# Ordering the program of a two-layer hybrid backbone by another model of the engines

## The chip, the cores and the metric

The kernel runs on one core of one Trainium2 chip. A core has a matrix engine (TensorE, PE in the profile), three engines for element-wise work (VectorE or DVE, ScalarE or ACT, GpSimd or POOL), a queue for data transfers (SyncE, SP) and 16 DMA engines. Each engine works through its own list of instructions in the order in which the program puts them there; semaphores hold an instruction back until what it reads has been written. The metric is the device time of one execution in microseconds (us). Times are compared with the median of several runs.

## What is computed

Two layers are applied to 256 latent tokens and 256 context tokens of width 1024 (batch 1), in fp32. Each layer is a half-step SwiGLU FFN, a token mixer and another half-step FFN; every sub-layer is modulated (adaLN) by vectors that come from a condition vector and a large matrix `ada_w`.

```python
for l in range(DEPTH):                                     # DEPTH = 2
    mx = (silu(c) @ ada_w[l] + ada_b[l])                   # 9 modulation vectors per stream
    x = x + 0.5 * mx[2] * swiglu(ada_norm(x, norm_g[l, 0], mx[0], mx[1]), ffn_w_in[l, 0], ffn_w_out[l, 0])
    # the same for the context stream hctx
    hx, hc = ada_norm(x, ..., mx[3], mx[4]), ada_norm(hctx, ...)
    yx, yc = even_mixer(hx, hc, ...) if l % 2 == 0 else odd_mixer(hx, hc, ...)
    x = x + mx[5] * yx
    x = x + 0.5 * mx[8] * swiglu(ada_norm(x, norm_g[l, 2], mx[6], mx[7]), ffn_w_in[l, 1], ffn_w_out[l, 1])
    # the same for hctx, but not in the last layer
return rms_norm(x, final_g)
```

The even mixer is differential attention with 4 heads beside a bidirectional mLSTM with 4 heads; the odd mixer is bidirectional gated linear attention (GLA) with 4 heads. The hidden width of an FFN is 2816.

## The kernel before

The two token streams lie side by side as columns 0 to 255 (context) and 256 to 511 (latent) of tiles with 128 features in the partitions, so that most matmuls have 512 columns. Every large product is done in three passes over split numbers: a weight tile and an activation tile are each cut into a rounded high part and a rest, and `mm3` adds high x high, high x rest and rest x high into one bank (L146, L147, L148).

The stages follow each other in the code: `begin` (loads, transposes of the tokens, first modulation vectors), the first FFN, the even mixer, two FFNs, the odd mixer, the last FFN with the final norm.

How the work of a stage reaches the engines:

- `load` (L116) issues a 1 MB transfer of weights from SP's queue into one of three `raw` buffers. `ada_step` (L167) uses the same three buffers for quarters of `ada_w`.
- `split` cuts half of such a buffer: ACT copies it, rounded, into `whi` (L120), DVE subtracts that from the raw values into `wlo` (L121). There are two buffers of each, so ACT can begin on a half only when PE is done with the half before the last.
- In an FFN, `ffn_in` goes through 22 tiles of hidden features in pairs; for each tile PE does 48 matmuls from two halves, and `gated` forms silu(a) x b (ACT at L348 and L350, DVE at L349 and L351). After each pair, `ada` calls `ada_step` twice: eight multiply-adds of 128 x 1024 on DVE (L176, L178). `out_pass` does the second product of the FFN and calls `ada_step` once for each raw buffer. The calls stop when the 64 steps (16 units of modulation vectors by 4 quarters) are done.
- `norm_steps` and `modulate` form the normalised activations `hh` and `hl` for the next stage (ACT, DVE, and POOL at L275).
- The even mixer runs the gate chain of the mLSTM (L759 to L790: activations on ACT, scans on DVE, transposes by PE at L784), then the heads: scores, weights, their transposes (`wtrans`, L894), the product with the values (`pv`, L907), a norm, and the transpose of the result (L916). `stack` (L841 to L847) lays out queries and keys for the scores. Between the heads stand projections that are independent of them (`rows_pair` with L632 to L634, `qk_pair`, `opre_pair`).
- The odd mixer does the same with `decays` (transposes at L1202), `states` and `head_out` (products at L1258 and L1260, transposes at L1267).

What sets the order of the work: the code is traced once, and when the block `with tile.TileContext(...)` closes, a list scheduler puts the traced instructions into the queues. It goes through a modelled execution, and whenever an engine of the model is to get an instruction, it takes, of those whose inputs are there and whose buffers are free at that moment of the model, the one that stands first in the code. So an instruction can pass others of its engine that stand ahead of it in the code but are not ready by the model. It also hands out the buffers of a pool as the instructions come up. Semaphore waits are put in after that, and keep the result right whatever the order. Only `keep_in_program_order` (L107), used for loads of the activation tables, ties an instruction to the one traced before it on its engine. No cost, due time or priority is written by hand.

## Time and profile before

| what | us |
|---|---|
| median of 3 runs | 1805.3 |
| lowest and highest | 1801.82 and 1805.34 |
| the profiled execution | 1805.46 |
| its span, first to last instruction | 1803.8 |

The profiled execution takes 1.7 us more than its span, for what lies around the program's own instructions. The profile's page is made from this one execution. Its mean granted PE clock is 0.995.

How to read it: a row of a group names the line of the kernel, the engine, the operation, and what it writes and reads (out<-in, buffer numbers left out), then the count, the busy time and the mean duration of one. "SPq" is SP's queue, in which an issue of a transfer can wait. A wait is put down to the engine whose result came last. PE's ends are modelled, and successive matmuls overlap in the rows, so that start-to-start distances say more of its pace than durations do.

The transfers are large and many, and in these rows of the page (line, engine, count, KB each, us from issue to landing) the largest are seen:

```profile
raw<-in_ffn_w_in_dram SPq DMA_DIRECT2D x84, 1024.0 KB, 5.3
raw_ada<-in_ada_w_dram SPq DMA_DIRECT2D x64, 1024.0 KB, 5.0
raw<-in_ffn_w_out_dram SPq DMA_DIRECT2D x41, 1024.0 KB, 5.0
```

The lines on which the argument rests stand in the prediction.

### The profile page before, as it was taken

The page shows a single profiled execution, that of the slowest core. Times are in us where ns is not written, and L with a number is a line of the kernel's source. Part 1 is how long each engine was busy: PE and PEld are TensorE (multiplying, and loading weights), DVE is VectorE, ACT ScalarE, POOL GpSimd, SP SyncE. Part 2 cuts the span into 40 slices and gives each one's busy share as a digit, 9 for nine tenths or more (in the row PEclk, how much of TensorE's full clock was granted, in tenths as well). Part 3 has the DMA queues.
Part 4 walks back from the last instruction along what each step waited for, and adds up shares of the span by engine and source line. Part 5 has one row for each costly group of instructions (what it writes and reads, how often), then busy time and mean ns, then how long its engine had stood idle before and what let it go on. Part 6 is the DMA issues. An engine that isn't in the chain of part 4 may idle for free.

```text
span 1803.8 us, 24901 instructions
## 1 busy us (share of the span) xinstructions
PE 1765.4 (98%) x10087; PEld 1503.6 (83%) x10087; DVE 1153.9 (64%) x1678; ACT 743.3 (41%) x1286; POOL 107.1 (6%) x172
## 2 busy tenths in 40 slices
PE   8999999999999999999999999999999999999998
PEld 5777778899887788777788897777888998899996
DVE  5767775657669866677753486777543747855555
ACT  4422222237658853222222352222222656654443
POOL 1000000013011020000000010000000200010000
PEclk9999999999999999999999999999999999999999
DMA  9555545443121214555542344555443632235553
GB/s 295 177 187 179 177 158 192 164 132 122 47 71 47 94 48 140 182 175 182 184 142 97 129 141 163 187 187 187 140 133 101 189 117 71 89 106 191 186 190 117
DMA packets 209303, 262.30 MB, mean 145 GB/s; under 512 B 6863, under 2 KB 188662, under 8 KB 209188
## 3 DMA queue, kind: packets, MB, share of 16 engines
q1 hardware_dynamic: 208160, 259.28, 44.0%
q8 instruction: 79, 1.29, 0.3%
q0 software_dynamic: 576, 0.84, 0.2%
q10 hardware_dynamic: 452, 0.59, 0.1%
q14 instruction: 36, 0.29, 0.1%
HBM read 259.64 MB, written 1.05 MB: 145 GB/s over the span
## 4 chain that ended last, share of the span: by engine, by line
PE 85%; DVE 7%; ACT 4%; issue 2%; DMA 1%; SPq 0%; POOL 0%; ACTq 0%; POOLq 0%; DVEq 0%
PE ps_ab L146 16%; PE ps_ab L147 16%; PE ps_ab L148 16%; PE ps_y L146 7%; PE ps_y L148 7%; PE ps_y L147 7%; PE ps_fm L148 2%; PE ps_fm L146 2%; PE ps_fm L147 2%; DVE wlo L121 1%; PE po L907 1%; PE ada_ps L190 1%; PE ps_l L1382 1%; PE ps_l L1383 1%; PE ps_l L1381 1%
## 5 line engine op out<-in xcount | busy, mean ns | idle before, releaser
L120 ACT CAST whi<-raw 128x1024 fp32r<-128x1024 f32 (+1 forms) x326 | 336.0, 1031 | 849.7 <-PE ps_ab L147 497.3
L121 DVE TENSOR_TENSOR wlo<-raw,whi 128x1024 fp32r<-128x1024 f32 (+1 forms) x326 | 392.6, 1205 | 314.4 <-ACT whi L120 309.5
L146 PE MATMUL ps_ab<-hh,whi 128*128 128x512 f32 (+1 forms) x1360 | 491.3, 362 | 1.8 <-ACT whi L120 1.0
L147 PE MATMUL ps_ab<-hl,whi 128*128 128x512 f32 (+1 forms) x1360 | 490.4, 361 | 2.6 <-POOL hl L275 2.3
L148 PE MATMUL ps_ab<-hh,wlo 128*128 128x512 f32 (+1 forms) x1360 | 489.4, 360 | 0.4 <-DVE wlo L121 0.3
L178 DVE SCALAR_TENSOR_TENSOR acc<-raw_ada,cs,acc 128x1024 f32<-128x1024 f32 x224 | 276.5, 1280 | 42.8 <-DMA raw_ada<-in_ada_w_dram 42.8
L146 PEld LDWEIGHTS ps_ab<-hh,whi 128*128 128x128 f32 x1360 | 255.4, 188 | 50.1 <-ACT whi L120 6.3
L147 PEld LDWEIGHTS ps_ab<-hl,whi 128*128 128x128 f32 x1360 | 255.9, 188 | 46.0 <-POOL hl L275 2.9
L148 PEld LDWEIGHTS ps_ab<-hh,wlo 128*128 128x128 f32 x1360 | 255.7, 188 | 44.0 <-DVE wlo L121 1.0
L148 PE MATMUL ps_y<-gh,wlo 128*128 128x512 f32 (+1 forms) x660 | 229.9, 348 | 0.4
L146 PE MATMUL ps_y<-gh,whi 128*128 128x512 f32 (+1 forms) x660 | 230.0, 348 | 0.0
L147 PE MATMUL ps_y<-gl,whi 128*128 128x512 f32 (+1 forms) x660 | 228.8, 347 | 0.0
L148 PEld LDWEIGHTS ps_y<-gh,wlo 128*128 128x128 f32 x660 | 124.9, 189 | 17.7 <-DVE wlo L121 1.6
L349 DVE TENSOR_TENSOR s<-ps_ab,s 128x512 f32<-128x512 f32 (+1 forms) x88 | 54.7, 623 | 132.6 <-PE ps_ab L148 131.1
L146 PEld LDWEIGHTS ps_y<-gh,whi 128*128 128x128 f32 x660 | 124.9, 189 | 17.1 <-ACT whi L120 1.2
L147 PEld LDWEIGHTS ps_y<-gl,whi 128*128 128x128 f32 x660 | 124.9, 189 | 15.5
L257 POOL TENSOR_TENSOR ssum<-ssum,sq 128x256 f32<-128x256 f32 x25 | 26.2, 1049 | 1117.8 <-ACT sq L255 842.2
L146 PE MATMUL ps_fm<-hh,whi 128*128 128x256 f32 (+1 forms) x256 | 83.8, 327 | 0.0
L148 PE MATMUL ps_fm<-hh,wlo 128*128 128x256 f32 (+1 forms) x256 | 83.2, 325 | 0.0
L147 PE MATMUL ps_fm<-hl,whi 128*128 128x256 f32 (+1 forms) x256 | 82.9, 324 | 0.0
L632 PE MATMUL ps_v<-whi,hh 128*128 128x256 f32 x256 | 73.4, 287 | 1.3 <-ACT mv L636 1.3
L633 PE MATMUL ps_v<-wlo,hh 128*128 128x256 f32 x256 | 73.9, 289 | 0.0
(375 smaller groups left out, 2383.4 us busy)
## 6 DMA issues: line engine op xcount, KB each, us to landing
raw<-in_ffn_w_in_dram SPq DMA_DIRECT2D x84, 1024.0 KB, 5.3
raw_ada<-in_ada_w_dram SPq DMA_DIRECT2D x64, 1024.0 KB, 5.0
raw<-in_ffn_w_out_dram SPq DMA_DIRECT2D x41, 1024.0 KB, 5.0
raw<-in_even_w_in_dram SPq DMA_DIRECT2D x12, 1024.0 KB, 5.3
raw<-in_odd_w_in_dram SPq DMA_DIRECT2D x12, 1024.0 KB, 5.4
raw<-in_ffn_w_out_dram SPq DMA_DIRECT2D x15, 768.0 KB, 4.3
raw_c<-in_ada_w_dram SPq DMA_DIRECT2D x16, 512.0 KB, 7.4
raw<-in_even_w_out_dram SPq DMA_DIRECT2D x4, 1024.0 KB, 5.0
```

The source lines that it names most:

```text
L120: nc.scalar.copy(hi3, r3)
L121: eng.tensor_tensor(lo3, r3, hi3.bitcast(F32), ALU.subtract)
L146: nc.tensor.matmul(ps, lhsT=wh, rhs=ah, start=first, stop=False)
L147: nc.tensor.matmul(ps, lhsT=wh, rhs=al, start=False, stop=False)
L148: nc.tensor.matmul(ps, lhsT=wl, rhs=ah, start=False, stop=last)
L178: nc.vector.scalar_tensor_tensor(ada_acc[i], r3[:, k2], s, ada_acc[i], ALU.mult, ALU.add)
L190: nc.tensor.matmul(ps[32 * j : 32 * j + 32, :256], lhsT=unit_e[:, 2 * (n - first) + i], rhs=acc[i][:, j * 256 : j * 256 + 256], start=n == ...
L257: (nc.gpsimd if i and k < KC - 2 else nc.vector).tensor_tensor(ssum[i][0], ssum[i][0], sq, ALU.add)
L349: nc.vector.tensor_tensor(s[:, sl], ps[1][:, sl], s[:, sl], ALU.mult)
L632: nc.tensor.matmul(o, lhsT=ah, rhs=wh[:, k4], start=k == 0 and t % 2 == 0, stop=False)
L633: nc.tensor.matmul(o, lhsT=ah, rhs=wl[:, k4], start=False, stop=False)
L907: nc.tensor.matmul(po[:, t], lhsT=w[:, kt, (t % 2) * P : (t % 2) * P + P], rhs=v[:, kt, h * P : h * P + P], start=kt == 0, stop=kt == nk - 1,)
```

## The change

`TileContext` is given `schedule_with_timeline_sim=True`. The list scheduler then goes through its modelled execution on another model of the core: the timeline model, in which each instruction is a series of steps (decoding, waiting in the engine's queue, executing, its result and its semaphore landing later) that hold parts of an engine for their own times, in place of the core model, in which an instruction takes its engine for one length of time. When an instruction is ready, and when its engine can take it, comes out at other moments, and so may the order of the instructions within each engine's queue and the buffer that a tile is given. The instructions themselves, their shapes and the numbers they compute stay the same.

```diff
@@ -1445,7 +1445,7 @@
             nc.dram_tensor(f"in_{name}_dram", a.shape, mybir.dt.from_np(a.dtype), kind="ExternalInput").ap()
         )
     args.append(nc.dram_tensor("out_0_dram", _OUT, F32, kind="ExternalOutput").ap())
-    with tile.TileContext(nc) as tc:
+    with tile.TileContext(nc, schedule_with_timeline_sim=True) as tc:
         backbone_kernel(tc, *args)
     r = _run(nc, [arrays], core_ids=[0])
     return r.results[0]["out_0_dram"].reshape(1, T, D)
```

## The prediction

> **What bounds the kernel now.** First the page: the span, the busy times, and the chain of work that ended last.
>
> ```profile
> span 1803.8 us, 24901 instructions
> PE 1765.4 (98%) x10087; PEld 1503.6 (83%) x10087; DVE 1153.9 (64%) x1678; ACT 743.3 (41%) x1286; POOL 107.1 (6%) x172
> PE 85%; DVE 7%; ACT 4%; issue 2%; DMA 1%; SPq 0%; POOL 0%; ACTq 0%; POOLq 0%; DVEq 0%
> ```
>
> TensorE (PE) is busy for 1765.4 of 1803.8 us and carries 85% of the chain. No order of the same instructions can win more than the 38.4 us in which PE does nothing, and that is 2.1%. So I next ask where these 38.4 us lie, with the view of busy time by stretches (columns: length, then busy time of PE, PEld, DVE, ACT and POOL, the granted PE clock, the DMA share and GB/s).
>
> ```profile
> 0.00:50.00 50.00, 41.81 (x255) 30.35 (x259) 27.23 (x73) 20.17 (x42) 4.99 (x23) 0.93 1.05 297
> 50.00:400.00 350.00, 350.00 (x1687) 282.69 (x1680) 230.96 (x262) 103.36 (x138) 5.52 (x5) 1.00 0.51 169
> 400.00:700.00 300.00, 286.46 (x1902) 255.38 (x1901) 228.88 (x493) 202.82 (x464) 47.50 (x70) 0.99 0.25 78
> 700.00:1000.00 300.00, 300.00 (x1354) 239.98 (x1353) 180.00 (x194) 81.78 (x105) 3.28 (x3) 1.00 0.48 159
> 1000.00:1100.00 100.00, 98.83 (x649) 90.13 (x648) 63.30 (x82) 44.09 (x71) 10.20 (x10) 1.00 0.43 143
> 1100.00:1400.00 300.00, 300.00 (x1366) 240.94 (x1366) 177.02 (x194) 81.54 (x107) 5.07 (x5) 1.00 0.47 154
> 1400.00:1700.00 300.00, 292.85 (x2325) 279.71 (x2324) 191.50 (x316) 164.61 (x298) 27.91 (x55) 1.00 0.42 133
> 1700.00:1750.00 50.00, 50.00 (x366) 47.46 (x366) 26.99 (x32) 24.00 (x32) 0.00 (x0) 1.00 0.54 188
> 1750.00:1804.00 54.00, 45.46 (x200) 36.99 (x198) 28.01 (x39) 20.93 (x32) 2.64 (x2) 0.97 0.37 135
> ```
>
> The four FFN stretches (50 to 400, 700 to 1000, 1100 to 1400, 1700 to 1750) are 1000 us with no idle PE at all. The idle time is 8.2 us at the start, 13.5 us around the even mixer (400 to 700), 1.2 us at 1000 to 1100, 7.2 us around the odd mixer (1400 to 1700) and 8.5 us at the end. The third view, PE's waits, says what the mixers wait for: first 400 to 700, then 1400 to 1700 (columns: total us, times, longest).
>
> ```profile
> PE pmt L784 <- DVE t L781: 3.3, 1, 3.3
> PE pt L894 <- DVE ea L974: 2.2, 2, 1.4
> PE pt_o L916 <- DVE on L913: 1.6, 2, 1.4
> ...
> PE pt L894 <- DVE E L882: 1.1, 3, 0.4
> PE ptg L1202 <- DVE kd L1178: 2.9, 5, 0.9
> PE po L1260 <- ACT st L1249: 1.3, 2, 0.8
> ...
> PE pt_o L1267 <- DVE on L1263: 0.2, 1, 0.2
> ```
>
> These are the links of the heads' own chains: PE wants a transpose or a product, and the DVE or ACT result before it is not there. Everything else in the mixers is covered: while one head's link is under way, PE has projection matmuls of other heads to run.
>
> **The change part by part.** No instruction, tile or shape is added or removed; what moves is the order in each engine's queue and, with it, which instruction gets a shared buffer first. So the sum has one kind of term: waits that go and waits that come, stage by stage.
>
> *FFN stretches, 1000 us.* The timeline of DVE, ACT and PE here:
>
> ```profile
> 149.30 4.87 DVE L178 SCALAR_TENSOR_TENSOR acc<-raw_ada,cs,acc 128x1024 f32<-128x1024 f32 x4
> 154.09 1.21 DVE L121 TENSOR_TENSOR wlo<-raw,whi 128x1024 fp32r<-128x1024 f32 x1
> 146.48 1.05 ACT L120 CAST whi<-raw 128x1024 fp32r<-128x1024 f32 x1 [4.04 <-issue]
> 152.08 1.05 ACT L120 CAST whi<-raw 128x1024 fp32r<-128x1024 f32 x1 [3.99 <-PE ps_ab L147]
> 152.07 0.40 PE L146 MATMUL ps_ab<-hh,whi 128*128 128x512 f32 x1
> 152.53 0.40 PE L148 MATMUL ps_ab<-hh,wlo 128*128 128x512 f32 x1
> ```
>
> One half-tile of weights costs PE 5.60 us (152.08 - 146.48, one cast per half). The cast at 152.08 fills the buffer for the half that starts 5.60 us later, at 157.68, and its wlo is first read 0.46 us into that half (152.53 - 152.07), at 158.14. The wlo ends at 155.30 although four adaLN multiply-adds (4.87 us) stood in front of it. That leaves 2.84 us: two more multiply-adds (1.22 us each) may slip in front without PE noticing, a third may not. Lower end: below nothing is excluded, because PE has no idle time here to give. Upper end: four further multiply-adds in front, 4.87 - 2.84 = 2.0 us for each of the 64 adaLN steps (16 units by 4 quarters in the code), 130 us. I take 0, since the rows nearest to this, today's, already have a whole step of four in front and still 2.84 us in hand.
>
> SP's queue of loads moves too, if the buffers come free in another order:
>
> ```profile
> SPq L116 <- DVE wlo L121: 844.2, 127, 22.3
> ```
>
> SP stands waiting for a raw buffer nearly half of the time, so it issues a load as soon as there is room, and the loads have no other input to wait for. The DMA share is about half (0.47 to 0.51 above). I take 0 for it; if a weight load came one adaLN step late (4.87 us), the same 2.84 us would cover more than half.
>
> *Start and end, 16.7 us idle.* The start waits for loads and the end is one dependent chain behind the last matmul; neither has other ready work to put in between. I take 0, with ends of -2 and +2 us (a quarter of the start's 8.2 us).
>
> *The mixers.* In the code a head of the even mixer has three transposes of weights (L894) and one of the output (L916), with 8 heads 32 links; the odd mixer has 8 transposes at L1202, 4 products at L1260 and 4 transposes at L1267, 16 links. Of the 48, the rows above show 15 that wait (2 + 2 + 3 + 5 + 2 + 1) for 2.2 + 1.6 + 1.1 + 2.9 + 1.3 + 0.2 = 9.3 us, 0.62 us each. The other 33 are covered. Another model places the filling matmuls elsewhere. Lower end: all 15 are covered, -9.3 us. Upper end: all 48 are bare, 33 x 0.62 = +20.5 us. I take half of them bare, 24 of 48: 9 more than now, 9 x 0.62 = +5.6 us. Why half: the order is fixed before the run, and at each link the real times differ from the modelled ones by some tenths of a us, in one direction or the other, so that a link is late about as often as early; today's 15 of 48 is better than that, and a new order has 33 links to lose and 15 to win.
>
> One wait can be traced to an order that is visibly unlucky. The gate chain of the mLSTM (L760 to L781) ends in the 3.3 us wait at L784:
>
> ```profile
> 443.75 0.69 ACT L760 ACTIVATE t<-psg,gb 64x512 f32<-64x512 f32 x1
> 444.46 0.62 ACT L845 CAST stk<-mq 64x512 fp32r<-64x512 f32 x1
> 445.10 0.63 ACT L761 ACTIVATE t<-t 64x512 f32<-64x512 f32 x1
> 445.76 0.62 ACT L844 CAST stk<-mq 64x512 fp32r<-64x512 f32 x1
> 446.40 0.72 ACT L762 ACTIVATE t<-t,one_t 64x512 f32<-64x512 f32 x1
> ...
> 450.00:455.00 5.00, 2.25 (x19) 2.04 (x18) 4.82 (x7) 1.57 (x2) 0.12 (x1) 1.00 0.00 0
> 455.00:460.00 5.00, 4.46 (x23) 4.27 (x24) 3.84 (x8) 2.06 (x7) 0.40 (x1) 0.66 0.00 0
> ```
>
> Two copies that the gate chain does not need (0.62 us each) stand between three links of it: 1.2 us of the wait is order, and the new order may keep or drop them. Both ends, 0 and -1.2; I take 0, for the timeline shows no reason why another model would not fill the same gaps. The last two rows are stretches: after the wait PE was granted 0.66 of its clock for 5 us, which costs (1 - 0.66) x 5 = 1.7 us more. This is the one place in the mixers where a wait costs more than its length.
>
> [...]
>
> **The sum** is 0 + 0 + 5.6 = +5.6 us on the profiled execution. Its own time is 1805.5 us, 1.7 us around the span, and that is the median of the runs shown (1805.3). Forecast: 1811 us.
>
> **The rivals.**
> *Better cover (faster).* The times of the timeline model are nearer to the engines' own, and the mixers' links are covered. All 15 waits and the 1.2 us of the gate chain go: 1805.5 - 9.3 - 1.2 = 1795 us; with the clock dip too, 1793. For it: most waits are under 1 us, the size of a wrong estimate of one DVE operation. Against it: 33 links of 48 are already right.
>
> *Nothing that can be measured.* The new order differs in places that are covered, or is the old one: 1805.5 us. For it: 1000 us without idle PE, and 2.8 us in hand at each half. Against it: the rows of the gate chain show copies written far behind it in the code standing inside it, so the order does hang on modelled times to tenths of a us. Of changes within 0.2% (3.6 us) a measurement of this kernel can't tell whether they are there; its three runs differ by that much.
>
> *The adaLN work runs ahead (slower).* If the timeline model lets ready instructions into DVE's queue before DVE is free, two adaLN steps stand in front of a wlo: eight multiply-adds where four stand now, and PE waits 2.0 us (worked out above). It decides from the third extra multiply-add on. At a quarter of the 64 steps that is 16 x 2.0 = 32 us, 1838 us; at an eighth 1822. For it: DVE is busy for 231 of 350 us in the first FFN stretch, the most of all engines beside PE. Against it: three raw buffers are shared by weights and adaLN, so two adaLN loads are seldom in at once. [...]
>
> **How the numbers follow.** Forecast (half of the links bare, 1809 to 1817): 0.30. Better cover (1790 to 1802): 0.30. Nothing that can be measured: 0.22. AdaLN ahead (1820 and more): 0.18. Faster by over 0.2%: 0.30; within: 0.22; slower: 0.30 + 0.18 = 0.48. The likeliest single case and the likelier side agree on slower, but the cases of the other sign hold much: its own range is 1809 to 1817. The range for 8 in 10 goes from 1791 to 1838: it leaves out the far ends of the two outer cases, about a tenth on each side, since each may be wider than I could price it.
>
> **What would show it.** Right: the FFN stretches still have 300 of 300 and 350 of 350 us of PE; PE's idle time at 400 to 700 and 1400 to 1700 rises from 20.7 to about 26 us; the waits at L894, L916, L1202 and L1260 become more in number, not longer. Wrong towards faster: fewer than 15 such waits, and no copies (L844, L845) between L760 and L762. Wrong towards slower: PE waiting for wlo L121 or whi L120 in ps_ab, in runs of about 2 us, with eight multiply-adds of L178 in a row ahead; or a granted clock under 1 in more stretches than the one above. The forecast falls altogether if the loads on SP's queue come in another order and PE waits for raw.

## The result, and the profile after

| | us | runs |
|---|---|---|
| before | 1805.32 (1801.82 to 1805.62) | 4 |
| after | 1886.34 (1882.53 to 1890.53) | 4 |
| ratio | 1.0453 (1.044 to 1.0466) | |

The changed kernel is 81 us slower. The forecast was +5.6 us, and the time lies far outside the range. The profiled execution of the changed kernel took 1887.84 us. Its page (span, busy times, chain of work that ended last):

```profile
span 1886.1 us, 24938 instructions
PE 1796.1 (95%) x10087; PEld 1526.4 (81%) x10087; DVE 1157.2 (61%) x1678; ACT 744.6 (39%) x1286; POOL 107.9 (6%) x172
PE 81%; DVE 8%; DMA 4%; ACT 3%; issue 2%; SPq 1%; POOL 0%; DVEq 0%; POOLq 0%; ACTq 0%
```

The instruction counts of the engines are those of before. The span grew by 82.3 us, in two parts: PE is busy for 30.7 us more with the same 10087 matmuls (1796.1 - 1765.4), and it does nothing for 51.6 us more (90.0 against 38.4). DVE's and ACT's busy times are the same to 3.3 and 1.3 us. The stretches say where; their bounds are moved so that each ends at nearly the same point of the work as in the table of before (columns as there; by the matmuls counted, to within some 30 of them):

```profile
0.00:50.00 50.00, 36.92 (x227) 27.37 (x227) 24.86 (x66) 18.68 (x38) 4.98 (x23) 0.90 0.99 279
50.00:410.50 360.50, 358.53 (x1714) 286.91 (x1711) 231.06 (x268) 104.78 (x139) 7.07 (x5) 1.00 0.50 166
410.50:760.50 350.00, 304.33 (x1917) 272.49 (x1916) 233.52 (x493) 205.22 (x467) 46.09 (x70) 0.92 0.21 67
760.50:1061.60 301.10, 301.10 (x1344) 238.65 (x1343) 179.90 (x193) 81.54 (x105) 3.34 (x3) 1.00 0.47 158
1061.60:1161.60 100.00, 95.00 (x617) 86.12 (x616) 57.23 (x77) 41.43 (x68) 8.74 (x10) 0.97 0.43 139
1161.60:1471.20 309.60, 309.60 (x1391) 246.36 (x1390) 182.01 (x197) 84.36 (x109) 4.72 (x5) 1.00 0.45 151
1471.20:1779.70 308.50, 292.50 (x2306) 281.42 (x2305) 192.34 (x315) 162.33 (x296) 29.92 (x55) 0.98 0.40 126
1779.70:1832.40 52.70, 52.70 (x389) 50.13 (x388) 28.33 (x34) 25.36 (x34) 0.00 (x0) 1.00 0.58 198
1832.40:1886.10 53.70, 45.47 (x200) 36.95 (x198) 27.94 (x39) 20.91 (x31) 2.99 (x2) 0.97 0.38 136
```

Third row: the stretch around the even mixer, 300 us before, now takes 350, with 45.7 us idle instead of 13.5, and the granted clock is 0.92 instead of 0.99. Rows 4 and 6: the FFN stretches are still without idle PE; the sixth is longer for the most part because more matmuls fall in it (1391 against 1366), left over from the row ahead of it. Around the odd mixer (row 7) 16.0 us are idle instead of 7.2. Rows 1 and 2, up to the even mixer, lost about 10 us, rows 5 and 6 together another 9.6, the end nothing.

PE's waits of after, the longest groups (total us, times, longest):

```profile
PE pt_o L916 <- DVE on L913: 14.8, 5, 3.6
PE pt_o L1267 <- DVE on L1263: 10.0, 3, 4.9
PE pt L894 <- DVE E L882: 9.6, 2, 6.1
PE pmod L524 <- DMA raw_c<-in_ada_w_dram: 6.0, 2, 3.5
PE pt L894 <- DVE ea L974: 5.0, 1, 5.0
PE ps_fm L148 <- DVE wlo L121: 4.4, 3, 3.6
PE ps_v L632 <- ACT mv L636: 4.3, 1, 4.3
```

The links at L894 and L916 waited 7 times before for 4.9 us; now they wait 8 times for 29.4 us. **There are hardly more waits; each is five times as long.** In the whole execution PE now stands still 11 times for 3.3 us or more, 45.2 us together; before it did so once. Around some of them (busy time by stretches):

```profile
429.70:434.00 4.30, 4.23 (x20) 4.23 (x21) 3.42 (x10) 0.00 (x0) 2.82 (x6) 0.50 0.73 225
588.00:592.00 4.00, 1.09 (x6) 0.69 (x6) 1.63 (x6) 1.75 (x7) 0.00 (x0) 1.00 0.00 0
592.00:596.00 4.00, 2.79 (x7) 1.70 (x7) 1.99 (x6) 3.95 (x13) 0.00 (x0) 0.53 0.00 0
596.00:600.00 4.00, 0.50 (x3) 0.32 (x3) 3.61 (x18) 3.00 (x9) 0.00 (x0) 0.50 0.00 0
```

The first row follows a wait of 3.56 us for a wlo that ended at 429.77: the granted clock is 0.50 in the 4.3 us behind it. The others show a mixer that has run out of covering work: of the 12 us from 588 to 600 PE is busy for 4.4, at a granted clock of 0.53 and 0.50 from 592 on. That is the longer busy time: the same matmuls at a lower clock. Over the whole span the shortfall of the mean granted clock grew from 9 us (0.005 x 1803.8) to 43 us (0.023 x 1886.1), which holds the 30.7 us.

**How a link becomes late.** The first link of the first mLSTM head, in the timeline of after (start, duration):

```profile
490.50 0.88 DVE L882 SCALAR_TENSOR_TENSOR E<-E,den 128x256 f32<-128x256 f32 x2
...
491.35 0.40 PE L148 MATMUL ps_fm<-hh,wlo 128*128 128x512 f32 x1
491.58 0.39 PE L146 MATMUL ps_fm<-hh,whi 128*128 128x512 f32 x1
...
494.85 0.39 PE L148 MATMUL ps_fm<-hh,wlo 128*128 128x512 f32 x1
495.07 0.60 PE L894 MATMUL pt<-ident,E 128*128 128x128 f32 x4
```

and in that of before:

```profile
466.44 0.28 PE L632 MATMUL ps_v<-whi,hh 128*128 128x256 f32 x1
466.58 1.54 DVE L882 SCALAR_TENSOR_TENSOR E<-E,den 128x256 f32<-128x256 f32 x3
467.11 0.44 PE L894 MATMUL pt<-ident,E 128*128 128x128 f32 x2 [0.39 <-DVE E L882]
```

In after the attention weights are there at 491.38 (490.50 + 0.88), and PE transposes them at 495.07, 3.7 us later. It isn't waiting: 15 projection matmuls (491.58 to 494.85), which nobody is waiting for, stand ahead in its queue. In before PE stops projecting and takes the transposes as soon as E lands. Over the 12 links at L882 of the four mLSTM heads, the time from the end of DVE's last piece to PE's first transpose was 0.7 us in sum before; in after the first six took 3.7, 4.0, 4.2, 2.3, 3.0 and 4.3 us, with 15 to 23 matmuls between, 22.6 us in sum (worked out from the rows of L882 and L894). So two things go together: the heads fall behind, and the projections, which were to cover the later links, are used up early. When the second head's output is transposed, 742 of the 864 projection matmuls of the stage's input (ps_fm and ps_v) are issued, against 475 before. From 580 us on the links stand bare.

So after the result the question was: what put those 15 to 23 matmuls in front, and which of the two, the lag or the early use of the cover, costs the time?

### The profile page after: what moved, and what is told of

It reads as the page before. It is cut to its first block, busy times and chain, and to the rows that moved or that the text cites. A ratio compares the mean times of both kernels' runs of the same rounds, so it can differ in the third digit from the quotient of the medians.

```text
span 1886.1 us, 24938 instructions
## 1 busy us (share of the span) xinstructions
PE 1796.1 (95%) x10087; PEld 1526.4 (81%) x10087; DVE 1157.2 (61%) x1678; ACT 744.6 (39%) x1286; POOL 107.9 (6%) x172
## 3 DMA queue, kind: packets, MB, share of 16 engines
HBM read 259.64 MB, written 1.05 MB: 138 GB/s over the span
## 4 chain that ended last, share of the span: by engine, by line
PE 81%; DVE 8%; DMA 4%; ACT 3%; issue 2%; SPq 1%; POOL 0%; DVEq 0%; POOLq 0%; ACTq 0%
PE ps_ab L148 14%; PE ps_ab L147 14%; PE ps_ab L146 14%; PE ps_y L148 6%; PE ps_y L146 6%; PE ps_y L147 6%; DMA raw_ada<-in_ada_w_dram 3%; PE ps_fm L148 2%; PE ps_fm L147 2%; PE ps_fm L146 2%; PE ps_v L632 2%; PE ps_v L633 2%; PE ps_v L634 2%; DVE wlo L121 1%; DVE acc L178 1%
## 5 line engine op out<-in xcount | busy, mean ns | idle before, releaser
L148 PE MATMUL ps_ab<-hh,wlo 128*128 128x512 f32 (+1 forms) x1360 | 492.0, 363 | 0.8 <-DVE wlo L121 0.7
L148 PEld LDWEIGHTS ps_ab<-hh,wlo 128*128 128x128 f32 x1360 | 256.4, 189 | 49.6 <-DVE wlo L121 5.7
L148 PE MATMUL ps_y<-gh,wlo 128*128 128x512 f32 (+1 forms) x660 | 230.8, 350 | 1.1 <-DVE wlo L121 1.0
L148 PEld LDWEIGHTS ps_y<-gh,wlo 128*128 128x128 f32 x660 | 124.9, 189 | 19.8 <-DVE wlo L121 2.9
L148 PE MATMUL ps_fm<-hh,wlo 128*128 128x256 f32 (+1 forms) x256 | 84.2, 330 | 4.5 <-DVE wlo L121 4.4
L632 PE MATMUL ps_v<-whi,hh 128*128 128x256 f32 x256 | 73.3, 288 | 4.3 <-ACT mv L636 4.3
```

The costliest lines, as they stand in the source:

```text
L148: nc.tensor.matmul(ps, lhsT=wl, rhs=ah, start=False, stop=last)
L632: nc.tensor.matmul(o, lhsT=ah, rhs=wh[:, k4], start=k == 0 and t % 2 == 0, stop=False)
```

## The experiments

Four theories stood at one time or another. *Queue room*: the timeline model hands an engine instructions as long as its modelled queue has a free place (35 entries for PE and 12 for each other engine in the changed kernel, which are settings of the scheduler's model: no run measures a queue of the chip; a matmul is two instructions, its weight load and itself, 10087 of each on the page), so the order is committed up to 17 matmuls before PE gets there (the counts of 15 to 23 above go a little beyond that room, so it isn't the whole of the lag). *Durations*: the timeline model's times or latencies are wrong for this kernel, whatever its queues. *Cover spent early*: the early use of the projections is the cause. *Loads*: the order of the loads does it. All times below are medians; ratios are to the kernel before on the same chip, with their 95% interval. Only sp_before, q12_1 and mix came out within a range that had been written down for one of their theories; the other nine lie outside all of theirs, so what they show is read from how far apart they lie.

| run | change to | us | ratio |
|---|---|---|---|
| d1_all | after, all queues 1 place | 2028.47 | 1.1243 (1.1226 to 1.126) |
| d1_rest | after, PE 35, others 1 | 1855.71 | 1.0288 (1.0271 to 1.0305) |
| q12_1 | after, PE 12, others 1 | 1833.36 | 1.0164 (1.0146 to 1.0182) |
| q4_1 | after, PE 4, others 1 | 1806.2 | 1.0016 (1.0005 to 1.0026) |
| q4_12 | after, PE 4, others 12 | 1823.41 | 1.0112 (1.0094 to 1.013) |
| core_peafter | before, PE's order of after | 1901.81 | 1.0536 (1.0513 to 1.0559) |
| tl_pebefore | after, PE's order of before | 1852.79 | 1.0266 (1.0251 to 1.0281) |
| tl_pebefore_d1r | the same, others 1 place | 1834.59 | 1.018 (1.0162 to 1.0198) |
| sp_before | after, SP's order of before | 1885.12 | 1.0448 (1.0432 to 1.0464) |
| hold | after, projections held back | 1900.72 | 1.0542 (1.0526 to 1.0558) |
| hold_d1r | the same, others 1 place | 1872.35 | 1.0374 (1.035 to 1.0398) |
| mix | before, two stages of q4_1 | 1797.58 | 0.9964 (0.9951 to 0.9976) |

### Whose order it is: PE's, the other engines', or the loads

An engine's order is pinned by a chain of dependencies that only order instructions and add no wait (the names come from the other kernel's program, shortened here):

```diff
     with tile.TileContext(nc) as tc:
         backbone_kernel(tc, *args)
+        _seq = {"PE": [169, 183, 190,
...
+        _all = {i.name: i for i in tc.nc.cur_bb.bb.instructions}
+        for _l in _seq.values():
+            _l = [f"I-{n}" for n in _l if f"I-{n}" in _all]
+            for _a, _b in zip(_l, _l[1:]):
+                tc.add_manual_dep(
+                    _all[_b], _a,
+                    mybir.DependencyInfo(mybir.DependencyClass.NoSync, mybir.DependencyReason.DATA), reason="order",
+                )
```

> The core model, as in the kernel before, but PE's instructions are held to the order that they have in the changed kernel; the other engines are ordered by the core model around that. If PE's order carries the loss: 1870 to 1890 us. If the loss is in the order of ACT and DVE: 1805 to 1825 us.

> The timeline model, but PE's instructions are held to the order of the kernel before. If PE's order carries the loss: 1803 to 1820 us. If the order of ACT and DVE carries it: 1860 to 1886 us.

> The changed kernel with SP's transfers held to the order of the kernel before; that order differs in 4 transfers, two of them in the start, where the changed kernel issues the third load of FFN weights ahead of a chunk of the adaLN matrix. If that is what costs the 9.3 us in the start's first product: 1875 to 1879 us. If it is PE's order: 1884 to 1889 us.

With PE's order of after alone the loss is all there, 97 us. The even mixer as one stretch, from its first projection matmul to the next FFN's first, in before:

```profile
411.80:671.10 259.30, 248.32 (x1610) 218.70 (x1609) 194.40 (x444) 179.28 (x419) 36.07 (x60) 0.99 0.23 70
```

The same stretch in after:

```profile
422.30:731.60 309.30, 265.06 (x1611) 234.54 (x1610) 196.25 (x439) 178.71 (x416) 35.32 (x58) 0.91 0.19 59
```

And in core_peafter:

```profile
421.40:737.70 316.30, 264.90 (x1610) 232.83 (x1609) 194.25 (x441) 178.20 (x415) 38.22 (x58) 0.92 0.18 58
```

The same 1610 matmuls (1611 records in after) take 259.3, 309.3 and 316.3 us, at a granted clock of 0.99, 0.91 and 0.92. The other engines' order costs too: with PE's order of before, tl_pebefore still loses 48 us. The two don't add up (97 + 48 against 81): the two orders of after lose less together than PE's alone beside the core model's order of the rest. The loads are out of it: their order differed in four transfers only, and putting it back leaves the time within the interval of after. The 9.3 us lost in the first product of the first FFN come with PE's order (core_peafter +9.5, tl_pebefore +1.5, sp_before still +8.9).

### How far ahead the model commits

The depth of the modelled queues is one table; each run changes this line (here d1_all):

```diff
+    from concourse import hw_specs as _hs
+    _d = _hs.TRN2Spec.ENG_ISSUE_QUEUE_DEPTH
+    _hs.TRN2Spec.ENG_ISSUE_QUEUE_DEPTH = {e: 1 for e in _d}
     with tile.TileContext(nc, schedule_with_timeline_sim=True) as tc:
```

For the others the last line reads, d1_rest and q4_1:

```diff
+    _hs.TRN2Spec.ENG_ISSUE_QUEUE_DEPTH = {e: n if e == mybir.EngineType.PE else 1 for e, n in _d.items()}
...
+    _hs.TRN2Spec.ENG_ISSUE_QUEUE_DEPTH = {e: 4 if e == mybir.EngineType.PE else 1 for e in _d}
```

with 12 in place of 4 in q12_1, and 12 in place of 1 in q4_12.

> The timeline model, but with every engine's queue in the model one instruction deep (PE 35 and ACT, DVE, POOL, SP 12 in the changed kernel). Theory A (the model takes instructions ahead of a busy engine, so that filling matmuls are placed in front of links of the heads' chains): 1800 to 1820 us, and PE's waits at L894, L916 and L1267 fall from 39 us to under 15. Theory B (the model's durations and landing times are what misplaces the instructions, whatever the depth): 1870 to 1890 us.

> The timeline model with the queues of ACT, DVE, POOL and SP one deep, PE's still 35. Theory A, if it is PE's depth that does it: 1870 to 1890 us. Theory A, if it is the depth of ACT and DVE (links late because ACT and DVE have other work in front): 1800 to 1825 us. Theory B: 1870 to 1890 us, as for all.

> The timeline model with PE's queue 4 deep, the others 12 as in the changed kernel. If PE's depth carries the mixers' loss by itself: 1830 to 1855 us. If it is the depth of ACT and DVE: 1870 to 1890 us.

> The timeline model with PE's queue 4 deep and all others 1 deep. If a deep PE queue is what puts projections ahead of the heads' links, and depth 1 was too shallow only because the modelled PE then no longer streams: 1815 to 1840 us, with PE's waits for wlo in ps_ab under 3 us. If a shallow PE queue spoils the FFN stretches as at depth 1: above 1900 us, with waits for wlo in ps_ab of tens of us.

> The timeline model with PE's queue 12 deep and the others 1 deep (1806.2 us at 4 deep, 1855.7 at 35). Theory E (an instruction that becomes ready has to go behind everything that the modelled PE queue already holds; with 35 places these were 15 to 23 matmuls or up to 4.3 us per link, with 4 places 2 to 7 or about 1 us): links of L894 in the mLSTM heads late by 1 to 2 us behind 5 to 9 matmuls, time in between, 1812 to 1835 us. A threshold instead of a proportion: 1806 or 1856 us.

d1_all was a miss: 2028 us, where queue room expected a time near before. One place does end the lag of the links at L882 (0 us in sum), but not the loss. Of the 223 us by which the execution is longer than before, 131 lie in the FFNs, 51 in the even mixer and 36 in the odd one. PE's waits of d1_all, some of the longest groups:

```profile
PE ps_ab L148 <- DVE wlo L121: 57.5, 16, 6.7
PE ps_y L148 <- DVE wlo L121: 19.3, 10, 3.3
PE ps_v L632 <- DVE ga L774: 14.6, 1, 14.6
...
PE pt_o L916 <- DVE on L913: 10.4, 8, 2.2
PE pt L894 <- DVE E L882: 9.4, 5, 3.4
```

With 5.6 us behind L974 and 5.1 us at L1267 the links of the heads still wait 30.5 us, where under 15 were expected. The even mixer takes 310.3 us, as long as in after, although PE takes up its links at once and its projections are used up hardly sooner than in before (447 issued at the second head's output, 475 in before). So neither the lag nor the early use of the cover explains the mixers of d1_all, and what does stays open. In the FFNs PE waits for wlo. The timeline of d1_all in the first of them:

```profile
146.25 3.67 DVE L178 SCALAR_TENSOR_TENSOR acc<-raw_ada,cs,acc 128x1024 f32<-128x1024 f32 x3 [6.67 <-DMA raw_ada<-in_ada_w_dram]
149.85 1.22 DVE L121 TENSOR_TENSOR wlo<-raw,whi 128x1024 fp32r<-128x1024 f32 x1
151.12 0.80 PE L148 MATMUL ps_ab<-hh,wlo 128*128 128x512 f32 x1 [6.11 <-DVE wlo L121]
```

DVE stands for 6.67 us in front of an adaLN multiply-add whose load isn't there, then does three (3.67 us), and only then the wlo for which PE waits 6.11 us. It is near the prediction's slow rival, but with a worse price and another cause: not multiply-adds that are ready, but one that waits for its transfer. Why one modelled place for PE leads to that order the runs don't show; that a queue of one place no longer streams in the model is argued, not shown.

With PE's 35 places kept and the others cut to 1 (d1_rest) part of the loss goes. The 2 x 2 of PE 35 or 4 and others 12 or 1 then settles the weights: PE from 35 to 4 places gains 62.9 us with the others at 12 (1886.3 to 1823.4) and 49.5 us with the others at 1 (1855.7 to 1806.2); the others from 12 to 1 gain 30.6 and 17.2 us. And it is graded: with the others at 1, PE at 4, 12 and 35 places gives 1806, 1833 and 1856 us, and the lag of the 12 links in sum 7.5, 17.9 and 24.7 us, with 4 to 7, 7 to 11 and 16 to 20 matmuls in front of each of the first five links. The part of the other engines' queues is not in this lag (6.5 us in q4_12, 7.5 in q4_1); where it sits was not traced. The even mixer of q4_1, by the same stretch:

```profile
415.40:679.40 264.00, 251.66 (x1610) 224.52 (x1609) 193.36 (x443) 178.09 (x416) 37.90 (x58) 0.97 0.22 69
```

Of q12_1:

```profile
418.00:697.80 279.80, 255.98 (x1610) 227.87 (x1609) 192.55 (x440) 178.57 (x414) 39.65 (x58) 0.96 0.21 65
```

Of d1_rest:

```profile
421.50:709.20 287.70, 259.43 (x1611) 229.77 (x1610) 190.57 (x438) 176.78 (x415) 37.58 (x57) 0.93 0.20 63
```

264.0, 279.8 and 287.7 us for the same matmuls; the granted clock falls with it, 0.97, 0.96 and 0.93. The model's durations are the same in all three, so they alone can't be the cause: with 4 places for PE and 1 for the others the timeline model's order takes as long as the core model's, to 2.2 us. With one place for PE too it does not (d1_all), so this holds from 4 to 35 places and not at one.

### Is it the early use of the cover?

hold leaves after as it is, but a projection that in before stood behind a head's output transpose may not be issued ahead of it:

```diff
     with tile.TileContext(nc, schedule_with_timeline_sim=True) as tc:
         backbone_kernel(tc, *args)
+        _hold = {"3876": [4047, 4048, 4049,
...
+        for _t, _l in _hold.items():
+            for _n in _l:
+                tc.add_manual_dep(
+                    _all[f"I-{_n}"], f"I-{_t}",
+                    mybir.DependencyInfo(mybir.DependencyClass.NoSync, mybir.DependencyReason.DATA), reason="order",
+                )
```

> The changed kernel (timeline model, all depths as they are) with one restriction on PE's order in the two mixers: a projection matmul (ps_v, ps_fm, ps_y) may not stand ahead of a head's output transpose (L916, L1267) that it stood behind in the kernel before. Nothing else is held. Theory C (the changed order spends the projections early, so that the late heads' chains have nothing beside them): 1825 to 1845 us, the stretch from the first ps_fm of the even mixer to the next ps_ab goes from 309 us back to 260 to 275. Theory D (PE waits because ACT and DVE serve the heads late, whatever PE has beside them): 1870 to 1890 us.

> The same restriction on the timeline model with the queues of ACT, DVE, POOL and SP one deep (1855.7 us without it). If theory C and the depth of ACT and DVE add up: 1815 to 1835 us. If the shallow queues already took away what the restriction takes away: 1845 to 1860 us.

It got worse, 1900.7 us, outside both ranges. The projections are spread as before, and the output transposes at L916 now follow their norm almost at once (1.0 us of lag in sum over 8 heads, 8.1 in after). But the links at L882 lag on (18.7 us against 22.6), and PE waits (even mixer of hold):

```profile
PE pt_o L916 <- DVE on L913: 19.1, 7, 5.2
PE pt L894 <- DVE E L882: 5.6, 4, 2.9
```

So what was kept for later doesn't help while the links stay late: the waits only move. With the others at one place (hold_d1r) it is 17 us slower than d1_rest, which holds nothing back. So the early use of the cover can't be mended by itself. That it is a consequence of the early commitment is argued: no run has prompt links together with projections used early.

### What is left, and a faster order

> The timeline model with PE's instructions held to the order of the kernel before and the queues of ACT, DVE, POOL and SP one deep (1852.8 us with these queues 12 deep). Theory E for the other engines too (what becomes ready goes behind up to 12 instructions that ACT or DVE already hold): 1805 to 1822 us. If the other engines' loss comes from the model's durations, or from a model of PE that is held up differently: 1840 to 1855 us.

tl_pebefore_d1r is tl_pebefore with the table of d1_rest. Of the 48 us that the other engines' order costs beside PE's order of before, the depth of their queues explains 18 (1852.8 to 1834.6). The other 30 lie in the even mixer (+13.5 us) and the odd one (+9.8) for the most part. Where they come from stays open: those engines' order was made for another order of PE, and no run separates that from the model's durations.

mix is the kernel before with every engine's order pinned to what it was, but the instructions of the second FFN and of the odd mixer stand among themselves as in q4_1, which had been faster in those two stretches. Its edit is the pin shown above, with all five engines in `_seq`.

> The core model, with all engines held to one order: that of the kernel before, except that the instructions of the second FFN and of the odd mixer take among themselves the order of the timeline model with queues of 4 and 1 (in which those two stretches were 4.0 and 4.2 us shorter than before). If the gains of the stretches carry over: 1795 to 1799 us. If they hang on how the neighbouring stretches are ordered: 1802 to 1808 us.

1797.58 us (1794.72 to 1801.4), 0.9964 of before: a gain of 0.4%, small but with its interval below 1, and 89 us under the changed kernel. From its page:

```profile
span 1797.8 us, 24910 instructions
PE 1761.3 (98%) x10087; PEld 1503.0 (84%) x10087; DVE 1152.7 (64%) x1678; ACT 742.2 (41%) x1286; POOL 105.8 (6%) x172
```

The two stretches (the first product of the second FFN, and the odd mixer) gain 3.1 and 3.0 us, of the 4.0 and 4.2 by which they were faster in q4_1, and the even mixer is that of before to 0.1 us.

## Why the prediction was wrong, step by step

- **FFN stretches, 0:** right but for 2.0 us. PE is busy for 301.1 of 301.1 and 309.6 of 309.6 us in rows 4 and 6, and for 358.5 of 360.5 in row 2.
- **Loads, 0:** right. Their order changed in four places, and putting it back changes nothing that can be measured.
- **Start and end, 0 (ends of 2 us):** right at the end, wrong at the start. "Neither has other ready work to put in between" overlooked that PE's order decides there too: PE waits 6.0 us at L524 in after (two waits, one of 3.5 us), and the start and the first FFN product are 9.9 us longer together, which goes with PE's order and not with that of the loads. The joint from the second to the third FFN, with the first product of the third, had no term in the sum at all and cost as much.
- **Mixers, +5.6 us:** this is the step that failed. That covered links would come to lie bare was right; the number and the price of the bare ones were wrong, and so was the reason for them. "9 x 0.62 = +5.6 us" expected 24 waits in place of 15, "more in number, not longer"; after has 11, all at L894, L916 and L1267, 39.4 us (14.8 + 10.0 + 9.6 + 5.0). They are fewer and longer: 3.6 us each (39.4 / 11) for 0.62, and the term measured +30.1 us (39.4 - 9.3). The reason given, that a link is late "about as often as early" by some tenths of a us, gives no such length: the first six links at L882 are all late, by 2.3 to 4.3 us. That the sign came out as forecast is therefore in part luck. The 0.62 us was the mean of waits that are left when the cover is a few tenths of a us too short, not the price of a link without cover. That price could be read from before. In the timeline of before, from the last product of a head to the transpose of its normed output:

```profile
525.73 2.62 PE L907 MATMUL po<-mv,wT 128*128 128x128 f32 x22
...
531.14 0.69 DVE L913 TENSOR_TENSOR on<-po,rm 128x512 f32<-128x512 f32 x1
531.89 0.66 PE L916 MATMUL pt_o<-ident,on 128*128 128x128 f32 x4 [0.23 <-DVE on L913]
```

and the same in that of after:

```profile
651.92 1.05 PE L907 MATMUL po<-av,wT 128*128 128x128 f32 x8
...
656.51 0.66 PE L916 MATMUL pt_o<-ident,on 128*128 128x128 f32 x4 [3.54 <-DVE on L913]
```

The chain is 3.54 us in both (531.89 - 525.73 - 2.62 before; 656.51 - 651.92 - 1.05 after). Before covered 3.3 of it with projections and showed a wait of 0.23; after covers nothing, and shows all of it at four of the eight heads (3.54 to 3.63 us). With 3.54 us for each of the 33 covered links the upper end would have been 117 us, not 20.5, and the measured 81 lies inside it; as an upper end for a single link it is still too short, for some of L894 and L1267 waited 4.9 to 6.1 us.
- **Gate chain, 0:** the wait of 3.3 us at L784 is gone in after, a gain of 2.1 us more than the step's end of -1.2. Beside the rest it doesn't show.
- **Clock, 1.7 us behind the wait of 3.3 us:** near in size, and left out of the sum because no such wait was expected. In the even mixer PE is busy for 16.7 us more (265.06 - 248.32) with 9 waits of 3.5 us and more: at most 1.9 us each, by estimate (16.7 / 9). At most, for the clock was down behind shorter waits too: in after it was 0.52 from 643.5 to 647.0, right behind waits of 0.92 and 1.79 us, and in before 0.86 from 672 to 680, where the longest wait was 1.45 us. So the wait at L784 was not the only one that cost more than its length. The bound of 38.4 us on any gain left the clock out too: it took PE's busy time as fixed, but that is 30.7 us longer in after and 4.1 us shorter in mix.
- **What had no term:** of the 51.6 us of added idle time 30.1 are the links; the other 21.5 are waits that the sum didn't have, among them those of the start, of the joint behind the second FFN and of the first matmuls of a projection (4.3 us at L632, 4.4 at L148).
- **The slow rival** (ready instructions taken into a queue before the engine is free) named what the runs then showed, but put it at DVE and in the FFN, with 32 us at most. It decides at PE and in the mixers, where a link has to pass the queue: there a matmul of 512 columns ahead of it costs 0.23 us (491.58 - 491.35) and takes two of the modelled places, so that the setting of 35 places comes to 4.0 us of delay, by estimate (17.5 x 0.23), beside the 2.3 to 4.3 us by which the first six links were late. It had 0.18 of the chances. Its last sign, a granted clock under 1 in more stretches, came true (0.92, 0.97 and 0.98 in rows 3, 5 and 7).

What the trace of after, the pins and the depths show together: the timeline model's queue room, 35 entries for PE above all and 12 for the others, commits the order ahead of the moment when it matters, by 2.3 to 4.3 us at the first six links. Cutting PE's depth alone from 35 to 4 takes away 63 us of the 81, and cutting both leaves 2.2 us over before. At one place for all there is another loss (d1_all), whose cause is open.

## What to carry to other kernels

A static order is only as good as the moment at which it is decided: a scheduler that fills a modelled queue ahead puts work that nobody waits for in front of results that are about to land, and on an engine that is busy for 98% of the time this was paid twice here, in late chains first and in bare ones later. The depth is not to be cut without a measurement either: one place for all engines gave the slowest of all these runs. To price the loss of cover, take the length of the whole dependent chain from the last product to the next, not the length of the waits that today's cover leaves (here 3.54 us for 0.62). And read the granted clock of each stretch beside its waits: here the matmuls of the even mixer ran 16.7 us longer at 0.91 than at 0.99.

## What the runs showed of the hardware

The clock's part was larger than expected: the mean granted clock was 0.977 in after against 0.995 in before, and 30.7 us of the 82.3 us of span are the same matmuls running longer. Half the clock was granted for 4.3 us behind a single wait of 3.56 us in a stretch that was otherwise full.
